# One small DRAM-to-DRAM copy put ahead of the first load of an instance-norm kernel

## The chip, the cores and the metric

The kernel runs on one core of a Trainium2 chip. The metric is the device time of one execution in microseconds (us). Three runs of the kernel before gave 627.54, 626.73 and 627.55 us, so the median is 627.54 us. The profile is one further execution, recorded by the hardware profiler.

A core has four computing engines that matter here: TensorE (PE), VectorE (DVE), ScalarE (ACT) and GpSimd (POOL). A fifth, SyncE (SP), only issues transfers. Transfers between device memory (DRAM) and the on-chip memory are carried by 16 DMA engines. SP, ACT and POOL can each put transfers into a queue of their own; all queues are served by the same 16 DMA engines.

## The reference: what is computed

```python
def reference(x, gamma):
    B, G, C_per_g, H, W = x.shape            # 4, 8, 16, 256, 256, float32
    mu = x.mean(axis=(3, 4), keepdims=True)
    var = ((x - mu) ** 2).mean(axis=(3, 4), keepdims=True)
    x_norm = (x - mu) / np.sqrt(var + 1e-5)
    out = x_norm * gamma[None, :, :, None, None]
    return out.astype(np.float32)
```

There are 4 x 8 x 16 = 512 channels of 256 x 256 = 65,536 numbers. Each channel is normalized by its own mean and variance and multiplied by one number of gamma. The input is 134.2 MB and so is the output; each has to cross between DRAM and the chip once.

## The kernel before, in words

The input is cut into 32 units (`U`). A unit is 16 channels. Each channel is spread over 8 partitions (`S`), 8,192 numbers in each, so a unit is a tile of 128 partitions by 8,192 float32 numbers: 4 MB, 32 KB in a partition. In DRAM a unit is one contiguous stretch of 4 MB.

Six tiles of that size, the slots `xt0` to `xt5` (line 45), hold the units that are in flight (`AHEAD = 6`). A unit is loaded into a slot, normalized there in place, and stored from there.

At the start, the gamma vector is loaded by POOL (line 52). Then the first six units are loaded (lines 53 and 54, through `load`, line 47): units 1 and 3 by the ACT queue, units 0, 2, 4 and 5 by the SP queue. A few constants are made: the averaging matrix `navg` on POOL, and `g_col`, gamma spread over the partitions, by DVE and PE.

The loop from line 100 takes the units in order. For each unit:

- DVE sums each partition (line 102), while ACT sums the squares of each partition (line 103).
- PE adds the sums over the 8 partitions of each channel and divides by the size (line 111).
- Four tiny operations turn that into the factor `scale` (lines 112, 116, 120, 122).
- DVE subtracts the mean and multiplies, in place (line 125).
- ACT issues the store of the unit to `out` (line 129).
- SP issues the load of the unit six places later into the same slot (line 131). It has to wait until the store from that slot has landed.

The order of instructions on each engine is the order in which they are written (`manual_schedule`, line 43). The waits between engines are put in by the framework, from what each instruction reads and writes, DRAM tensors too. The ACT and SP transfers share eight completion semaphores in turn. A transfer that reuses a semaphore waits until the transfer that used it before has landed.

Of the kernel before, what the change touches and what calls it, by code (L numbers as in the profile page):

```python
# [1 line left out]

# [4 lines left out]

F32 = mybir.dt.float32
U8 = mybir.dt.uint8
ALU = mybir.AluOpType  # L10
ACTF = mybir.ActivationFunctionType
AX = mybir.AxisListType


@with_exitstack
def kernel(
    ctx: ExitStack,
    tc: tile.TileContext,
    x: bass.AP,
    gamma: bass.AP,  # L20
    out: bass.AP,
):
    nc = tc.nc
    B, G, C, H, W = x.shape
    P = nc.NUM_PARTITIONS
    HW = H * W
    n_ch = B * G * C
    S = 8
    K = P // S
    F = HW // S  # L30
    U = n_ch // K
    NG = (G * C) // K
    AHEAD = 6
    assert HW % S == 0 and (G * C) % K == 0

    xv = x.rearrange("b g c h w -> (b g c h w)").rearrange("(u p f) -> u p f", p=P, f=F)
    ov = out.rearrange("b g c h w -> (b g c h w)").rearrange("(u p f) -> u p f", p=P, f=F)
    gv = gamma.rearrange("g c -> (g c)")

    data = ctx.enter_context(tc.tile_pool(name="data", bufs=1))  # L40
    singles = ctx.enter_context(tc.tile_pool(name="singles", bufs=1))
    psum = ctx.enter_context(tc.tile_pool(name="psum", bufs=4, space=bass.MemoryType.PSUM))
    ctx.enter_context(tc.manual_schedule())

    slots = [data.tile([P, F], F32, name=f"xt{i}") for i in range(AHEAD)]

    def load(u, queue):
        queue.dma_start(out=slots[u % AHEAD][:], in_=xv[u])  # L48


    g_row = singles.tile([1, G * C], F32, name="g_row")
    nc.gpsimd.dma_start(out=g_row[:], in_=gv[None, :])  # L52
    for u in range(AHEAD):
        load(u, nc.scalar if u in (1, 3) else nc.sync)


    eps_t = singles.tile([P, 1], F32, name="eps_t")
    nc.gpsimd.memset(eps_t[:], 1e-5)  # L58
    one = singles.tile([1, 1], F32, name="one")
    nc.gpsimd.memset(one[:], 1.0)  # L60
    navg = singles.tile([P, K, S], F32, name="navg")
    nc.gpsimd.memset(navg[:], -1.0 / HW)  # L62
    nc.gpsimd.affine_select(  # L63
        out=navg[:], in_=navg[:], pattern=[[-S, K], [0, S]], compare_op=ALU.is_ge,
        fill=0.0, base=0, channel_multiplier=1,
    )
    nc.gpsimd.affine_select(  # L67
        out=navg[:], in_=navg[:], pattern=[[S, K], [0, S]], compare_op=ALU.is_ge,
        fill=0.0, base=S - 1, channel_multiplier=-1,
    )  # L70
    navg_w = navg[:].rearrange("p k s -> p (k s)")
    root_eps = singles.tile([P, 1], F32, name="root_eps")
    nc.scalar.activation(out=root_eps[:], in_=eps_t[:], func=ACTF.Sqrt)  # L73
    g_rep = singles.tile([1, NG, K, S], F32, name="g_rep")
    g_ps = psum.tile([P, NG], F32, name="g_ps", bufs=1)
    g_col = singles.tile([P, NG], F32, name="g_col")

    nc.vector.tensor_copy(  # L78
        out=g_rep[:],
        in_=g_row[:].rearrange("o (n k) -> o n k", n=NG).unsqueeze(3).to_broadcast([1, NG, K, S]),  # L80
    )
    for n in range(NG):
        nc.tensor.matmul(  # L83
            out=g_ps[:, n : n + 1],
            lhsT=g_rep[:, n].rearrange("o k s -> o (k s)"),
            rhs=one[:],
            start=True, stop=True,
        )
    nc.vector.tensor_copy(out=g_col[:], in_=g_ps[:])  # L89

    junk = singles.tile([P, F], U8, name="junk")

    st = singles.tile([P, U, 2], F32, name="st")
    nvar = singles.tile([P, U], F32, name="nvar")
    std = singles.tile([P, U], F32, name="std")
    rstd = singles.tile([P, U], F32, name="rstd")
    scale = singles.tile([P, U], F32, name="scale")

    squares = []
    for u in range(U):  # L100
        t = slots[u % AHEAD]
        nc.vector.reduce_sum(out=st[:, u, 0:1], in_=t[:], axis=AX.X)  # L102
        square = nc.scalar.activation(  # L103
            out=junk[:], in_=t[:], func=ACTF.Square, accum_out=st[:, u, 1:2],
        )
        if u:

            tc.declare_no_dep(square.ins, squares[-1].ins, reason="junk, ordered by the root between")
        squares.append(square)
        ps = psum.tile([P, 2], F32, name="ps")  # L110
        nc.tensor.matmul(out=ps[:], lhsT=navg_w, rhs=st[:, u], start=True, stop=True)  # L111
        nc.vector.tensor_scalar(  # L112
            out=nvar[:, u : u + 1], in0=ps[:, 0:1], scalar1=ps[:, 0:1],
            scalar2=ps[:, 1:2], op0=ALU.mult, op1=ALU.add,
        )
        nc.scalar.activation(  # L116
            out=std[:, u : u + 1], in_=nvar[:, u : u + 1], func=ACTF.Sqrt,
            bias=eps_t[:], scale=-1.0,
        )
        nc.vector.reciprocal(out=rstd[:, u : u + 1], in_=std[:, u : u + 1])  # L120
        g = u % NG
        nc.vector.tensor_mul(  # L122
            out=scale[:, u : u + 1], in0=rstd[:, u : u + 1], in1=g_col[:, g : g + 1],
        )
        nc.vector.tensor_scalar(  # L125
            out=t[:], in0=t[:], scalar1=ps[:, 0:1], scalar2=scale[:, u : u + 1],
            op0=ALU.add, op1=ALU.mult,
        )
        nc.scalar.dma_start(out=ov[u], in_=t[:])
        if u + AHEAD < U:  # L130
            load(u + AHEAD, nc.sync)


# [1 line left out]
_INS = ['x', 'gamma']  # L135
_OUTS = [((4, 8, 16, 256, 256), 'float32')]


# [23 lines left out]
```

## Time and profile before

| What | Value |
|---|---|
| Median of three runs | 627.54 us (626.73 to 627.55) |
| Span of the profiled execution, first to last instruction | 625.2 us |
| Median time less that span | 2.3 us |
| Bytes moved by all DMA engines | 268.46 MB |
| Mean rate over the span | 429 GB/s |
| Busy: DVE, ACT, PE, POOL | 443.2, 238.8, 21.4, 1.9 us |
| First loads issued (SP and ACT) | 0.81 us |
| First unit on the chip, DVE begins | 22.76 us |
| First store issued | 37.82 us |
| Last store issued | 600.59 us |

The profile gives no time of the profiled execution other than its span, so the span is what the profile is compared by; the median of the unprofiled runs lies 2.3 us above it.

The profile is read in microseconds from the start of the span. A group row names the line, the engine, the operation, what is written from what, how often it ran, its total and mean time, and the idle time of that engine just before it with what ended it. A row of the stretches view gives, for each stretch of the span, its length, the busy time of each engine, the granted TensorE clock, the share of time in which the DMA engines were busy, and the rate. A DMA packet is put down to the stretch in which it starts. A packet of this kernel is 32 KB, one partition of a unit, so stretches of one or two us are uneven by that alone.

### The profile page before, as it was taken

To read this page: it belongs to the slowest core of one execution; us is meant where nothing else is said; L and a number is where in the kernel's file an instruction comes from. 1 tells how busy PE (TensorE), PEld (TensorE's weight loads), DVE (VectorE), ACT (ScalarE), POOL (GpSimd) and SP (SyncE) were. 2 spreads that over 40 slices of the span, in tenths; PEclk is the share of its full clock that TensorE was granted. 3 is DMA by queue.
4 is the path that set the end of the run, shared out by engine and by line. 5 is a ranking of instruction groups with operands and counts; after the bars stand their busy time and mean duration, and the time that the engine had idled before them with its cause. 6 is when DMAs were issued, how large, how long until landed. Compare 5 with 4: busy or idle time off the path is not lost.

```text
span 625.2 us, 627 instructions
## 1 busy us (share of the span) xinstructions
PE 21.4 (3%) x80; PEld 19.6 (3%) x80; DVE 443.2 (71%) x162; ACT 238.8 (38%) x98; POOL 1.9 (0%) x10
## 2 busy tenths in 40 slices
PE   2000000000000000000000000000000000000000
PEld 2000000000000000000000000000000000000000
DVE  0588999999776687666786767867668676687730
ACT  0444444444443244432344423444224442244400
POOL 1000000000000000000000000000000000000000
DMA  8999999999999999999999999999999999999998
GB/s 369 436 403 436 436 436 436 436 426 432 434 434 436 424 434 436 436 434 436 436 421 434 434 434 432 432 434 436 436 434 436 436 419 434 434 436 432 432 434 369
DMA packets 9251, 268.46 MB, mean 429 GB/s; under 512 B 1057, under 2 KB 1057, under 8 KB 1057
## 3 DMA queue, kind: packets, MB, share of 16 engines
q10 hardware_dynamic: 4896, 142.61, 52.9%
q1 hardware_dynamic: 4320, 125.83, 46.8%
q14 instruction: 3, 0.02, 0.0%
q0 software_dynamic: 32, 0.00, 0.0%
HBM read 134.22 MB, written 134.22 MB: 429 GB/s over the span
## 4 chain that ended last, share of the span: by engine, by line
another core or an unknown queue 61%; DMA 17%; DVE 15%; SPq 1%; PE 1%; issue 0%; ACT 0%
DMA xt<-in_x_dram 10%; DVE st L102 10%; DMA out_dram<-xt 8%; DVE xt L125 5%; SPq L48 1%; PE ps L111 1%; ACT std L116 0%; DVE nvar L112 0%; DVE rstd L120 0%; DVE scale L122 0%
## 5 line engine op out<-in xcount | busy, mean ns | idle before, releaser
L102 DVE TENSOR_REDUCE st<-xt 128x1 f32<-128x8192 f32 x32 | 277.9, 8684 | 105.3 <-DMA xt<-in_x_dram 105.3
L103 ACT ACTIVATE junk<-xt 128x8192 uint8<-128x8192 f32 x32 | 224.9, 7029 | 275.4 <-DMA xt<-in_x_dram 232.2
L125 DVE TENSOR_SCALAR xt<-xt,ps,scale 128x8192 f32<-128x8192 f32 x32 | 145.6, 4550 | 1.2
L116 ACT ACTIVATE std<-nvar,eps_t 128x1 f32<-128x1 f32 x32 | 9.4, 294 | 79.7 <-DVE nvar L112 79.7
L111 PE MATMUL ps<-st,navg 128*128 128x2 f32 x64 | 17.9, 349 | 562.0 <-DVE st L102 562.0
L111 PEld LDWEIGHTS ps<-st,navg 128*128 128x128 f32 x64 | 16.1, 312 | 563.8 <-issue 563.8
L112 DVE TENSOR_SCALAR nvar<-ps 128x1 f32<-128x1 f32 x32 | 9.2, 287 | 23.9 <-PE ps L111 23.9
L120 DVE RECIPROCAL rstd<-std 128x1 f32<-128x1 f32 x32 | 5.3, 164 | 11.6 <-ACT std L116 11.6
L78 DVE COPY g_rep<-g_row 1x1024 f32<-1x1024 f32 x1 | 0.7, 683 | 10.6 <-DMA g_row<-in_gamma_dram 10.6
L103 ACT ACTIVATION_READ_ACCUMULATOR junk<-xt 128x1 f32 x32 | 6.0, 186 | 0.0
L122 DVE TENSOR_TENSOR scale<-rstd,g_col 128x1 f32<-128x1 f32 x32 | 5.1, 159 | 1.1
L83 PE MATMUL g_ps<-one,g_rep 1*128 1x1 f32 x16 | 3.5, 347 | 11.5 <-DVE g_rep L78 11.5
L83 PEld LDWEIGHTS g_ps<-one,g_rep 1*128 1x128 f32 x16 | 3.5, 326 | 11.4 <-issue 11.4
L89 DVE COPY g_col<-g_ps 128x8 f32<-128x8 f32 x1 | 0.2, 167 | 3.7 <-PE g_ps L83 3.7
L73 ACT ACT_TABLE_LOAD x1 | 1.3, 1283 | 1.7 <-PEq L146 1.7
L52 POOL DMA_DIRECT2D g_row<-in_gamma_dram x1 | 0.6, 607 | 0.8 <-POOLq L146 0.8
L63 POOL TENSOR_SCALAR_AFFINE_SELECT navg<-navg 128x128 f32<-128x128 f32 x1 | 0.4, 398 | 0.1
L67 POOL TENSOR_SCALAR_AFFINE_SELECT navg<-navg 128x128 f32<-128x128 f32 x1 | 0.4, 398 | 0.1
L62 POOL MEMSET navg<- 128x128 f32 x1 | 0.2, 230 | 0.0
L73 ACT ACTIVATE root_eps<-eps_t 128x1 f32<-128x1 f32 x1 | 0.2, 203 | 0.0
L58 POOL MEMSET eps_t<- 128x1 f32 x1 | 0.1, 118 | 0.0
L146 POOL MEMSET const-bfloat16-1.0<- 128x1 bf16 x1 | 0.1, 102 | 0.0
(4 smaller groups left out, 0.4 us busy)
## 6 DMA issues: line engine op xcount, KB each, us to landing
out_dram<-xt ACTq DMA_DIRECT2D x32, 4096.0 KB, 62.5
xt<-in_x_dram SPq DMA_DIRECT2D x30, 4096.0 KB, 38.5
xt<-in_x_dram ACTq DMA_DIRECT2D x2, 4096.0 KB, 31.8
g_row<-in_gamma_dram POOLq DMA_DIRECT2D x1, 0.5 KB, 9.3
```

What stands on the lines that cost most here:

```text
L48: queue.dma_start(out=slots[u % AHEAD][:], in_=xv[u])
L73: nc.scalar.activation(out=root_eps[:], in_=eps_t[:], func=ACTF.Sqrt)
L78: nc.vector.tensor_copy(out=g_rep[:], in_=g_row[:].rearrange("o (n k) -> o n k", n=NG).unsqueeze(3).to_broadcast([1, NG, K, S]),)
L83: nc.tensor.matmul(out=g_ps[:, n : n + 1], lhsT=g_rep[:, n].rearrange("o k s -> o (k s)"), rhs=one[:], start=True, stop=True,)
L102: nc.vector.reduce_sum(out=st[:, u, 0:1], in_=t[:], axis=AX.X)
L103: square = nc.scalar.activation(out=junk[:], in_=t[:], func=ACTF.Square, accum_out=st[:, u, 1:2],)
L111: nc.tensor.matmul(out=ps[:], lhsT=navg_w, rhs=st[:, u], start=True, stop=True)
L112: nc.vector.tensor_scalar(out=nvar[:, u : u + 1], in0=ps[:, 0:1], scalar1=ps[:, 0:1], scalar2=ps[:, 1:2], op0=ALU.mult, op1=ALU.add,)
L116: nc.scalar.activation(out=std[:, u : u + 1], in_=nvar[:, u : u + 1], func=ACTF.Sqrt, bias=eps_t[:], scale=-1.0,)
L120: nc.vector.reciprocal(out=rstd[:, u : u + 1], in_=std[:, u : u + 1])
L122: nc.vector.tensor_mul(out=scale[:, u : u + 1], in0=rstd[:, u : u + 1], in1=g_col[:, g : g + 1],)
L125: nc.vector.tensor_scalar(out=t[:], in0=t[:], scalar1=ps[:, 0:1], scalar2=scale[:, u : u + 1], op0=ALU.add, op1=ALU.mult,)
```

## The change

One transfer is added on the SP queue, ahead of its first load. It reads 16 pieces of 2 KB (512 numbers of each eighth partition row) from the first unit of `x` and writes them to the same places of the first unit of `out`. Nothing is computed from them. The first store, issued by ACT, writes the whole first unit of `out`, and so overwrites the pieces; as it writes the same DRAM bytes it now also waits for the copy. Nothing else is changed in the source.

```diff
     g_row = singles.tile([1, G * C], F32, name="g_row")
     nc.gpsimd.dma_start(out=g_row[:], in_=gv[None, :])
+    nc.sync.dma_start(out=ov[0][0::S, 0:512], in_=xv[0][0::S, 0:512])
     for u in range(AHEAD):
         load(u, nc.scalar if u in (1, 3) else nc.sync)
```

In the built program, SP has one instruction more, its first. The order of all other instructions on all engines is the same. The transfers of ACT and SP use the eight semaphores one place further on. The first store has one wait more.

## The prediction

> **What bounds the kernel now.** I read the page's busy shares and its 40 slices first, then the queues, the groups, the waits of the SP queue, and stretches of the span around the start and the first store. From the page:
>
> ```profile
> PE 21.4 (3%) x80; PEld 19.6 (3%) x80; DVE 443.2 (71%) x162; ACT 238.8 (38%) x98; POOL 1.9 (0%) x10
> DMA  8999999999999999999999999999999999999998
> GB/s 369 436 403 436 436 436 436 436 426 432 434 434 436 424 434 436 436 434 436 436 421 434 434 434 432 432 434 436 436 434 436 436 419 434 434 436 432 432 434 369
> q10 hardware_dynamic: 4896, 142.61, 52.9%
> q1 hardware_dynamic: 4320, 125.83, 46.8%
> ...
> L102 DVE TENSOR_REDUCE st<-xt 128x1 f32<-128x8192 f32 x32 | 277.9, 8684 | 105.3 <-DMA xt<-in_x_dram 105.3
> ...
> out_dram<-xt ACTq DMA_DIRECT2D x32, 4096.0 KB, 62.5
> xt<-in_x_dram SPq DMA_DIRECT2D x30, 4096.0 KB, 38.5
> xt<-in_x_dram ACTq DMA_DIRECT2D x2, 4096.0 KB, 31.8
> g_row<-in_gamma_dram POOLq DMA_DIRECT2D x1, 0.5 KB, 9.3
> ```
>
> The DMA engines are busy in every slice; DVE, the busiest computing engine, has 71% and waits for loads. The bytes set the time. What stands out is how few slices fall short of 434 to 436 GB/s: the first, the last, and the third (403), with no computing reason for the third. The stretches view looks closer:
>
> ```profile
> 0.00:1.50 1.50, 0.00 (x0) 0.00 (x0) 0.00 (x0) 0.00 (x0) 0.42 (x5) 1.00 0.00 0
> ...
> 35.00:40.00 5.00, 0.00 (x0) 0.00 (x0) 5.00 (x2) 1.78 (x1) 0.00 (x0) 1.00 1.02 433
> 40.00:44.00 4.00, 0.00 (x0) 0.00 (x0) 4.00 (x1) 4.00 (x1) 0.00 (x0) 1.00 1.07 377
> ...
> 300.00:500.00 200.00, 6.14 (x22) 5.52 (x22) 143.66 (x55) 76.67 (x33) 0.00 (x0) 1.00 1.00 433
> ```
>
> No byte moves in the first 1.5 us. Between 40 and 44 us the rate falls to 377 with the engines "busy" all along: packets take longer there. The timeline has the first store at 37.82 us, just ahead:
>
> ```profile
> 37.82 0.35 ACTq L129 DMA_DIRECT2D out_dram<-xt  x1
> ```
>
> The views sum the packet records; I took the records themselves (start and duration of each 32 KB packet; 8,192 of them, 512 rounds of one packet on each of 16 engines), turned to the span's clock and sorted by start, 16 to a round:
>
> ```
> round   earliest  latest   mean start (us)
> 0       1.811     2.950    2.183     first load packets, took 1.21 to 2.10 us
> 1       3.655     4.213    3.868
> 2       4.872     5.420    5.090
> 31      39.968    40.517   40.186    first store packets, took 1.21 to 2.08 us
> 32      41.461    42.166   41.761    load packets behind them, 1.38 to 2.14 us
> 33      43.272    43.878   43.483
> 511     621.717   622.676  622.180   took 1.21 us
> ```
>
> A round lasts 1.2095 us in the median. Two places lose time: from round 0 to 1, 1.685 us were taken (0.48 over); from round 31 to 33, 3.297 us (0.88 over, on every engine between 0.88 and 0.94). All 512 rounds are over by only 1.94 us together. So the time is 1.8 us until the first packet, 512 x 1.2095 = 619.3 us of packets, these stalls, the spread of the engines, and 1.3 us from the last packet's end (623.89) to the end of the span.
>
> **The change part by part.**
>
> Bytes. 16 pieces of 2 KB are one packet on each engine. At 32 KB in 1.21 us a piece is 0.08 us; read and written it is 0.15 at most.
>
> Issue on SP. The first four loads took SP 0.37, 0.43, 0.42 and 0.53 us to issue, so the copy pushes all of them 0.37 to 0.53 us back. The ACT load of unit 1 is issued at 0.81 us as before and feeds the engines meanwhile; later loads stand in rings that are never empty: 0. Were that cover gone, the price would be those 0.4 us once.
>
> New wait. The first store (37.82 us) waits for a copy issued at 0.81. Behind it on ACT stand the squares of unit 1, and SP's reload of slot 0. Even the slowest small transfer in the trace, gamma's 0.5 KB behind the loads, landed after 9.3 us; so the wait is over 27 us before it is asked for: 0. The semaphores shift by one place, but each transfer still follows the same predecessor (a store the store four before, a load an early load, the first reload the copy instead of a fresh semaphore); at the end too, the last stores wait as before: 0.
>
> The first-store stall. It is the first time that an engine writes to `out`, and no later store repeats it (the rounds after 33 take 1.20 to 1.24 us; the second store, issued at 52.76, shows nothing). I take it for the price of a first write to `out`, which the copy pays in its place: -0.88 us. Bounds: 0 if it is the price of mixing stores into loads, -0.94 as the largest seen.
>
> The start. Here the copy stands ahead of the loads, and no row shows a DRAM-to-DRAM packet. Before, the slowest engine ran as if it had begun at 3.00 us (its third packet at 5.42 less two rounds); the first load packets start spread over 1.14 us, from 1.81 to 2.95, which I read as a 128-row load being handed out row by row. The copy has 16 rows, so I let it begin on all engines at 1.81. It holds an engine for a first read (the earliest load packet was 1.896 long, 0.68 over), the first write (0.88) and the bytes (0.15): 1.71 us, until 3.52. Loads then start 0.52 us later than on the slowest engine before: +0.52. Bounds: 0, if loads pass the copy's stalled write or its hold is under 1.19; and the two longest packets of the trace in a row, 2.10 + 2.14 = 4.24, until 6.05: +3.05. I take the value between, as a piece of 2 KB waits for the same first accesses but has a sixteenth of their data.
>
> The Trainium skill, page "DMA: Bandwidth & Descriptors", section "Anatomy of one DMA — SWDGE (gpsimd) path", speaks against the change: any transfer has a fixed cost of about 2.0 us, mostly the wait for the memory's receipt of the last write. If all of that held the engines, the copy would last until 3.81 and the sum would be about -0.07; the same page's section "Rules for kernel authors" lets such a cost overlap with other work. No run here shows a copy's own yet.
>
> Sum: +0.52 - 0.88 = -0.36 us on a span of 625.2, so 624.8. The median of the runs lies 2.3 above the span (launch and end, untouched): 627.54 - 0.36 = 627.2.
>
> **The rivals.**
>
> *The copy hides in the wait for descriptors and takes the loads' first stall too (faster).* For it: half of the engines stood idle until 2.5 to 2.95 us, and the late ones had no stall in their first packet (1.21 us). Then 0.88 and 0.48 both go: -1.36, 626.2. Against it: the late engines set the end, and those lost nothing at the start; the gain would need load descriptors that come no later than before.
>
> *The copy holds the engines and cures nothing (slower).* Place: 1.8 to 4.8 us. The stall at 40 us belongs to the first packet that is read on chip and written to DRAM, so it stays; and the copy's packet takes as long as the longest first load, 2.10, with 0.88 behind it: until 4.79, +1.79, 629.3. It passes 0.2% (1.25 us, about what a measurement of this kernel can tell from no change) once the hold is over 2.44 us. For it: in the trace an engine's slow store packet also slows the load packet behind it, so a stalled write does block the engine. Against it: the copy does write DRAM, on the same 16 engines.
>
> *The stall stays, the copy is cheap (no change).* +0.52 by the hold above, 628.1. If the stall belonged to each unit's stretch of `out`, every store would show it, and only the first does; so this needs the first mixing of stores and loads as its cause, but they alternate for hundreds of further rounds without loss.
>
> **How the numbers follow.** The forecast has 0.50, its own range 626.6 (-0.94) to 627.9 (a hold of 2.0 and the spread of the medians, 0.8, shared to both sides). The faster rival has 0.17, the slower 0.20, the cheap copy without cure 0.13. Over 0.2% is below 626.3 or above 628.8. Faster: 0.17 and 0.03 of the forecast's low edge, 0.20. Slower: 0.20, with 0.02 of each of the other two, 0.24. Within: 0.56. The range runs from 626.0, just below the faster rival, to 629.1, which leaves out about half of the slower rival and the tail toward 630.6 (+3.05), together under 2 in 10.
>
> **What would show it.** In the profile after: the third slice back at some 430 GB/s or more and the stretch from 40 to 44 us (or the four us after the first store) at 433 instead of 377, if the first write was moved; packets of rounds 31 and 32 at 1.21. At the start, the copy's issue on SP, loads behind it about 0.4 us later, first unit on the chip some 0.5 us after 22.76. No wait of the first store on the copy. A landing of the copy after more than 2.5 us, or loads whose second round starts after 4.7, speaks for the slower rival. What would make me wrong: a copy that stalls an engine far longer than any packet here, or a stall at 40 us that no early write to `out` can take away.

## The result, and the profile after

The changed kernel has a median of 627.8 us (22 executions) against 627.2 us for the kernel before (22). The ratio of the two is 1.0023, with a 95% interval from 1.0013 to 1.0032. It is slower: the whole interval lies above 1. I had forecast 0.36 us less than before.

The medians differ by 0.6 us, and the ratio stands for 1.4 us, because the executions of the changed kernel spread in a way those of before do not. Its 22 have a mean of 628.55, those of before 627.12. Sixteen of them lie at 627.19 to 628.23, with a mean of 627.61 (0.49 over before), and six at 628.71 to 633.23, with a mean of 631.06. So of the 1.43 us between the means, 0.49 are the everyday loss, paid by the sixteen, and 0.94 come from the six, the tail. The highest of before's 22 is 627.55.

The profiled execution took 627.39 us, so it is one of the sixteen. From its page:

```profile
span 625.7 us, 629 instructions
...
PE 21.4 (3%) x80; PEld 19.5 (3%) x80; DVE 443.1 (71%) x162; ACT 238.9 (38%) x98; POOL 1.9 (0%) x10
...
GB/s 371 436 415 421 436 436 436 436 436 429 434 432 430 429 429 436 434 434 436 434 436 436 432 434 432 432 432 432 432 436 432 436 434 436 434 434 432 436 432 354
...
L103 DVE TENSOR_REDUCE st<-xt 128x1 f32<-128x8192 f32 x32 | 277.9, 8684 | 104.2 <-DMA xt<-in_x_dram 104.2
...
out_dram<-xt ACTq DMA_DIRECT2D x32, 4096.0 KB, 69.8
xt<-in_x_dram SPq DMA_DIRECT2D x30, 4096.0 KB, 30.3
xt<-in_x_dram ACTq DMA_DIRECT2D x2, 4096.0 KB, 26.9
out_dram<-in_x_dram SPq DMA_DIRECT2D x1, 32.0 KB, 7.8
g_row<-in_gamma_dram POOLq DMA_DIRECT2D x1, 0.5 KB, 7.2
```

The compute rows are what they were. The dent in the rate has not gone: it was in the third slice (403 GB/s) and is now spread over the third and the fourth (415 and 421), because the first store comes later. The copy itself landed 7.8 us after its issue. The last slice is lower, 354 instead of 369. The stores now take 69.8 us from issue to landing, not 62.5, and the SP loads 30.3, not 38.5: the backlog has moved from one queue to the other. The stretches view of the changed kernel around the first store:

```profile
35.00:40.00 5.00, 0.56 (x2) 0.50 (x2) 3.82 (x5) 0.34 (x2) 0.00 (x0) 1.00 0.97 419
40.00:44.00 4.00, 0.00 (x0) 0.00 (x0) 4.00 (x2) 0.62 (x1) 0.00 (x0) 1.00 0.97 418
44.00:49.00 5.00, 0.00 (x0) 0.00 (x0) 5.00 (x1) 5.00 (x1) 0.00 (x0) 1.00 1.06 393
300.00:500.00 200.00, 6.14 (x22) 5.51 (x22) 143.78 (x55) 74.48 (x31) 0.00 (x0) 1.00 1.00 434
```

The slow stretch is now 44 to 49 us (393 GB/s), right behind the issue of the first store. The timeline shows why it is there:

```profile
0.81 0.59 SPq L53 DMA_DIRECT2D out_dram<-in_x_dram  x1
0.82 0.87 ACTq L48 DMA_DIRECT2D xt<-in_x_dram  x2
...
1.46 2.25 SPq L48 DMA_DIRECT2D xt<-in_x_dram  x4
...
27.92 8.69 DVE L103 TENSOR_REDUCE st<-xt 128x1 f32<-128x8192 f32 x1 [14.87 <-DMA xt<-in_x_dram]
...
42.98 0.35 ACTq L130 DMA_DIRECT2D out_dram<-xt  x1
```

SP is 0.59 us busy with the copy, so ACT issues its load of unit 1 first, 0.6 us ahead of SP's load of unit 0. Unit 0 is on the chip at 27.92 us instead of 22.76, and the first store is issued at 42.98 instead of 37.82: both 5.2 us later. In the timeline before, both queues begin at once (SP's row takes in a reload that comes much later, hence its length):

```profile
0.81 0.89 ACTq L48 DMA_DIRECT2D xt<-in_x_dram  x2
0.81 62.13 SPq L48 DMA_DIRECT2D xt<-in_x_dram  x5
...
22.76 8.69 DVE L102 TENSOR_REDUCE st<-xt 128x1 f32<-128x8192 f32 x1 [7.55 <-DMA xt<-in_x_dram]
```

The packet records of the trace tell the rest. Sorted by start into rounds of one 32 KB packet per engine (times in us, mean start of the round), with the number of the 16 packets that belong to SP's queue:

```
          before                         after
round   start    of SP's queue        start    of SP's queue
0       2.183    16                   2.151    0
1       3.868    0                    4.083    0
2       5.090    16                   5.303    0
4       7.515    16                   7.819    0
30      38.977   16                   39.281   16
31      40.186   0  last of loads     40.491   16
33      43.483   0  first store       42.915   16
35      45.902   0                    45.338   16  first store next
36      47.112   16                   47.056   7
37      48.321   0                    48.423   9
100     124.649  16                   124.795  7
511     622.180  0                    622.294  0
```

Before, all 16 engines do the same thing in the same round: all load for SP, then all carry out ACT's packets (loads at first, stores later), and so on through the span. ACT's two loads are 256 packets, 16 on each engine, and fill its rounds up to 31. After, each engine takes five packets of ACT's queue first; the copy, one packet of 2 KB and 0.084 us on each engine, does not move before 6.05 us. ACT's two loads are used up with round 26, and rounds 27 to 35 are SP's alone. When the first store arrives, some engines take its packets one round sooner than others, and from then on 7 engines load while 9 store, and the other way round in the next round. I call that out of step; how many engines are in each group is the split.

The rounds also correct a reading of my prediction. Its round 31, put down as "first store packets", holds the last load packets of ACT's queue; the first store's packets begin in round 33 and take 1.21 us. So the stall of 0.88 us falls on load packets, in the two rounds ahead of the first store's. It does so in the other kernels too: in gap_no_copy, below, the slow rounds 30 and 31 (0.31 and 0.86 us too long) have no packet of ACT's queue at all. I go on calling it the stall of the first store, as it comes right ahead of that store's packets in all 16 profiles (0.57 to 1.18 us); what makes it is not shown.

### The profile page after: what moved, and what is told of

It reads as the page before. It is cut to its first block, busy times and chain, and to the rows that moved or that the text cites. A ratio compares the mean times of both kernels' runs of the same rounds, so it can differ in the third digit from the quotient of the medians.

```text
span 625.7 us, 629 instructions
## 1 busy us (share of the span) xinstructions
PE 21.4 (3%) x80; PEld 19.5 (3%) x80; DVE 443.1 (71%) x162; ACT 238.9 (38%) x98; POOL 1.9 (0%) x10
## 4 chain that ended last, share of the span: by engine, by line
DMA 50%; DVE 25%; another core or an unknown queue 18%; PE 1%; issue 0%; ACT 0%; SPq 0%
DMA xt<-in_x_dram 43%; DVE st L103 19%; DMA out_dram<-xt 8%; DVE xt L126 5%; PE ps L112 1%; ACT std L117 0%; DVE nvar L113 0%; SPq L48 0%; DVE rstd L121 0%; DVE scale L123 0%; SPq L53 0%
## 6 DMA issues: line engine op xcount, KB each, us to landing
out_dram<-xt ACTq DMA_DIRECT2D x32, 4096.0 KB, 69.8
xt<-in_x_dram SPq DMA_DIRECT2D x30, 4096.0 KB, 30.3
```

## The experiments

The first theory was that the *head start* of ACT's load harms, by the late unit 0. Its rivals were that the *copy itself* costs, wherever it is issued, and the *first-write* reading of my prediction. In all diffs, `for u in range(AHEAD)` is the loop of the first loads.

**The copy on POOL's queue (pool_copy).**

```diff
-    nc.sync.dma_start(out=ov[0][0::S, 0:512], in_=xv[0][0::S, 0:512])
+    nc.gpsimd.dma_start(out=ov[0][0::S, 0:512], in_=xv[0][0::S, 0:512])
```

> The same 16-piece copy, issued by POOL behind gamma instead of by SP; the first transfers of SP and ACT are as in the kernel before. Head-start theory (the copy harms by making SP's load of unit 0 come behind ACT's load of unit 1): unit 0 on the chip at 22 to 23.5 us, the stall of the first store (about 0.8 us) still there, time within 0.3 us of the kernel before, no executions of 630 us or more. Rival (a DRAM-to-DRAM copy costs by itself): 0.5 us or more over the kernel before, and some executions at 630 to 633 us as with the change. My prediction's first-write theory: the stall of the first store is gone, 0.9 us under the kernel before.

Measured: 626.92 us against 626.9, ratio 0.9998 (0.999 to 1.0007), highest execution 627.44. Unit 0 is on the chip at 22.70 us, and the rounds are whole (16 or 0). The stall of the first store is still there, 0.77 us over rounds 31 and 32; in the stretches view:

```profile
40.00:44.00 4.00, 0.00 (x0) 0.00 (x0) 4.00 (x1) 4.00 (x1) 0.00 (x0) 1.00 1.10 393
```

The copy costs nothing that this run can see (at most 0.4 us, by the interval) by its bytes, by its write or by the first store's wait. The first-write reading falls: `out` was written early, at 12.1 us, and the stall is as before.

**The copy on ACT's queue (act_copy).**

```diff
-    nc.sync.dma_start(out=ov[0][0::S, 0:512], in_=xv[0][0::S, 0:512])
+    nc.scalar.dma_start(out=ov[0][0::S, 0:512], in_=xv[0][0::S, 0:512])
```

> The same copy as ACT's first transfer instead of SP's. Head-start theory: now SP's load of unit 0 gets into the engines first, so unit 0 is on the chip earlier than before, at 16 to 20 us instead of 22.8, and the first store is issued by 35 us; time within 0.5 us of the kernel before and no executions of 630 us or more. Rival (the copy or one more transfer ahead of the loads costs by itself, on whichever queue): 0.5 us or more over the kernel before, with executions at 630 to 633 us.

Measured: 627.26 us, ratio 1.0005 (0.9996 to 1.0014), 626.98 to 627.46. Now SP's load has the head start: unit 0 is on the chip at 18.01 us, the first store is issued at 33.07, and the rounds stay whole. As the head-start theory has it. The median is 0.36 us over that of before, and the interval allows up to 0.9.

**A small load instead of the copy (sp_small_load).** The pieces go to a part of the tile `junk`, which is made earlier for it; nothing is written to `out`.

```diff
-    nc.sync.dma_start(out=ov[0][0::S, 0:512], in_=xv[0][0::S, 0:512])
+    junk = singles.tile([P, F], U8, name="junk")
+    scratch = junk[0:16, 0:2048].bitcast(F32)
+    nc.sync.dma_start(out=scratch, in_=xv[0][0::S, 0:512])
```

> SP's first transfer is again 16 pieces of 2 KB from x, but into a tile on the chip, so nothing is written to out and no store waits for it. Head-start theory: the same as the change, unit 0 at some 27 to 28 us, median about 0.6 us over the kernel before, and some executions at 630 to 633 us. Rival (the DRAM-to-DRAM copy or the first store's wait costs): as the kernel before, within 0.3 us, unit 0 may be late but no executions of 630 us or more.

Measured: 643.25 us, 641.09 to 644.99 in four executions, ratio 1.026 (1.0241 to 1.028). Neither theory had that. The small load moves at once, at 1.81 to 2.68 us, where the copy moved at 6.05 in the same place of the same queue, and at 6.05 in act_copy too; so its place on the queue does not by itself explain the copy's wait, and what does is not shown. SP's load of unit 0 is issued 0.42 us behind ACT's, and ACT's first three packets, not five, come first on every engine. Unit 0 is on the chip at 25.49 us. Up to the first store (40.55 us) the rounds are whole and no slower than in the changed kernel; behind it, they mix, at 11 to 5 first and at changing splits from 104 us on. From the page of the execution at 641.09 us:

```profile
span 639.4 us, 629 instructions
...
GB/s 373 437 406 426 441 433 426 424 426 443 428 426 427 431 435 431 426 424 428 433 435 431 420 431 428 439 426 422 426 433 435 426 424 431 428 435 424 428 433 117
```

The rate is a little low through the whole span, and the last slice is nearly empty. In the packet records, load packets over 1.24 us (1.38 us in the median) come again and again, 284 of them between 80 and 560 us; the kernel before has two. Through them the engines drift apart: the first have done all their packets at 623.9 us, the last at 637.8. A transfer waits for its slowest engine, so the drift is the time.

That gave the second theory, *out of step*: what costs is that some engines load while others store, and the start matters only by what it does to the step.

**Unit 0 on the queue with the head start (unit0_act).** The change, with this:

```diff
-        load(u, nc.scalar if u in (1, 3) else nc.sync)
+        load(u, nc.scalar if u in (0, 2) else nc.sync)
```

> The change, with ACT loading units 0 and 2 and SP the copy and units 1, 3, 4 and 5. Head-start theory: ACT's first load has the head start again, but it is now unit 0, so unit 0 is on the chip at 16 to 20 us; time within 0.5 us of the kernel before, no executions of 630 us or more. Rival (the copy on SP costs by itself): as the change, 0.6 us over with executions at 630 to 633 us.

Measured: 627.38 us, ratio 1.0007 (0.9998 to 1.0016), 627.08 to 627.97 in 11 executions. The copy is where the change has it, SP's first transfer. In the timeline the first unit and the first store are early:

```profile
18.10 8.69 DVE L103 TENSOR_REDUCE st<-xt 128x1 f32<-128x8192 f32 x1 [5.16 <-DMA xt<-in_x_dram]
...
33.15 0.35 ACTq L130 DMA_DIRECT2D out_dram<-xt  x1
```

The rounds stay whole, and no execution is over 628 us. The tail is not seen with the copy kept, though 11 executions are few for a tail of 6 in 22. Whether the everyday loss has gone too, the run does not tell: the median is 0.48 us over the one beside it (626.9), and the interval holds no change as well.

**The same undoing for the small load (small_unit0).** sp_small_load with the same edit of the loop, units 0 and 2 on ACT.

> As sp_small_load (643 us), SP's first transfer is 16 pieces of 2 KB into a tile on the chip, but ACT now loads units 0 and 2, so that the first store comes at about 33 us while ACT's queue is still busy or just ends. Out-of-step theory: rounds stay whole (0 or 16 packets of SP's queue) behind the first store and the 16 us are gone: 627 to 628 us. Rival (the small on-chip load itself is what costs, by the SP queue or by its place on the chip): still over 635 us.

Measured: 627.35 us, 627.21 to 627.39 in 10 executions, ratio 1.0004 (0.9994 to 1.0013). First unit at 20.64 us, first store at 35.70, rounds whole. The 16 us are gone though the small load is still there.

**The change again (after_again, after_look1, after_look2, after_look3).** No edit.

> The changed kernel once more, for its spread and another profile. Out-of-step theory (the late first store finds ACT's queue empty and enters the 16 engines in different rounds, so that from then on some engines load while others store, and this costs from nothing to several us): the median 0.4 to 1 us over the kernel before, and one execution in four at 628.5 to 634 us; a profile in which rounds of packets after 45 us mix the two queues. Rival (the extra cost is a fixed price of the start): all executions within 1 us of each other.

> The change once more for one profile, in search of an execution of its slow tail. Out-of-step theory: a profile over 628.5 us has, after the first store, rounds that mix the queues in another split than 7 to 9, and load packets over 1.24 us again and again through the span (over 2 us in sum per engine); a fast one has none after 60 us. Rival (the tail comes from the start): a slow profile loses its time in the first 60 us.

> A second profile of the change, to find an execution of its slow tail. Expected as for the first look: if over 628.5 us, mixed rounds of another split than 7 to 9 and load packets over 1.24 us through the whole span (out-of-step theory), or a loss in the first 60 us alone (rival: the start).

> A third profile of the change, to find an execution of its slow tail. Expected as for the first look: if over 628.5 us, mixed rounds of another split than 7 to 9 and load packets over 1.24 us through the whole span (out-of-step theory), or a loss in the first 60 us alone (rival: the start).

Measured: 12 further executions have a median of 627.55 us, ratio 1.0012 (1.0 to 1.0025), 627.18 to 628.11 but for one at 632.37; the tail is there, but rarer than one in four. The profiles: 627.61 us with a split of 7 to 9, 627.25 with 10 to 6, 629.87 with 8 to 8, 627.68 with 3 to 13. So the split changes from execution to execution. In the one at 629.87 us there are 122 load packets over 1.24 us between 80 and 560 us, which make 0.8 us an engine in the mean (over 2 was expected); in the three others two each. Its engines end between 623.5 and 626.6 us, those of the one at 627.25 between 622.9 and 623.9. The stretches view of the end, first of the execution at 629.87 us:

```profile
60.00:615.00 555.00, 16.73 (x60) 15.02 (x60) 412.37 (x150) 220.66 (x90) 0.00 (x0) 1.00 1.00 432
...
621.00:624.00 3.00, 0.00 (x0) 0.00 (x0) 0.00 (x0) 0.00 (x0) 0.00 (x0) 1.00 0.84 360
624.00:626.00 2.00, 0.00 (x0) 0.00 (x0) 0.00 (x0) 0.00 (x0) 0.00 (x0) 1.00 0.15 66
```

and of the changed kernel's first profile, 627.39 us:

```profile
60.00:615.00 555.00, 16.72 (x60) 15.01 (x60) 412.51 (x150) 220.87 (x90) 0.00 (x0) 1.00 1.00 433
...
621.00:624.00 3.00, 0.00 (x0) 0.00 (x0) 0.00 (x0) 0.00 (x0) 0.00 (x0) 1.00 0.58 251
624.00:626.00 2.00, 0.00 (x0) 0.00 (x0) 0.00 (x0) 0.00 (x0) 0.00 (x0) 1.00 0.00 0
```

After 624 us the one still carries packets, the other none. The long execution has the marks of sp_small_load in small. That fits the out-of-step theory and not the rival, a loss in the first 60 us. But the long one has a split of 8 to 8 and the others 7 to 9, 10 to 6 and 3 to 13, and all four are out of step, three of them at no such price, so neither being out of step nor the numbers of the split tell which execution is costly. What the two long profiled executions share is the slow load packets and a split that does not last: at 629.87 us it leaves 8 to 8 at 263 us, while in the others the same pattern goes on to the last loads.

**An early store from the chip (pool_store).** In place of the copy, POOL writes zeros from a tile (`scratch`, made as in sp_small_load) to the same pieces of `out`.

```diff
-    nc.sync.dma_start(out=ov[0][0::S, 0:512], in_=xv[0][0::S, 0:512])
+    nc.gpsimd.memset(scratch, 0.0)
+    nc.gpsimd.dma_start(out=ov[0][0::S, 0:512], in_=scratch)
```

> No copy; POOL stores 16 pieces of 2 KB of zeros from a tile on the chip to out's first unit at the start; the first store overwrites them. If the stall at the first full store (about 0.8 us around 40 us) is the price of an engine's first write to out from the chip, it is gone here (under 0.2 us). If it is the price of the first mixing of full stores into full loads, it stays at 0.7 to 1 us. Time within 1 us of the kernel before either way.

Measured: one execution, 627.02 us. The stall stays: rounds 31 and 32 take 0.33 and 0.50 us too long, 0.83 in sum. So it is not the first write to `out` from the chip either. It comes with the first full store, or with something else that the small transfers do not share; which, was not settled.

**ACT's queue empty without a copy (gap_no_copy).** The kernel before, with ACT loading unit 1 alone.

```diff
-        load(u, nc.scalar if u in (1, 3) else nc.sync)
+        load(u, nc.scalar if u in (1,) else nc.sync)
```

> The kernel before without any copy, but ACT loads unit 1 alone and SP units 0, 2, 3, 4 and 5, so ACT's queue runs empty at about 21 us, long before the first store (about 38 us). Out-of-step theory: rounds after the first store mix the two queues (neither 0 nor 16 packets of SP's queue in a round), and the time is as with the change or worse: 0.5 us or more over the kernel before, with executions at 629 us or more. Rival (the copy, or the head start of unit 1, is what costs): the first unit arrives as before, within 1 us of 22.8, and the time is within 0.3 us of the kernel before with no executions over 629 us.

Measured: 627.56 us, ratio 1.0008 (1.0 to 1.0017), 627.28 to 627.83 in 11 executions. First unit at 22.51 us as before. The rounds mix, but only at 15 to 1, and there is no tail. The median is 0.57 over before, so about as much as the everyday part of the change's loss appears with no copy; the tail does not. The stall is longer here, 1.18 us instead of 0.88.

**A late first store without a copy (late_store).** The kernel before, with DVE held up by 5.3 us ahead of unit 0.

```diff
+    nc.vector.reduce_sum(out=st[:, 0, 0:1], in_=slots[0][:, 0:4900], axis=AX.X)
     squares = []
```

> The kernel before, with no copy and all transfers in their old order; DVE reduces 4,900 columns of unit 0 once more before it begins (about 5.2 us, its result is overwritten), so that the first store is issued at about 43 us as with the change, 3 us after ACT's queue has run out of loads. Out-of-step theory: the first store splits the engines, rounds after 45 us mix the queues, and the time is 0.3 to 1.5 us over the kernel before, with an execution over 628.5 us now and then. Rival (the copy or the head start of unit 1 costs): within 0.2 us of the kernel before, as DVE has the time to spare, and no tail.

Measured: 627.08 us, ratio 1.0003 (0.9994 to 1.0012), 626.73 to 627.29 in 11 executions. The first store comes at 42.99 us, as with the change; the engines split 15 to 1. Less than the 0.3 us that the out-of-step theory had put as its least, and no tail. A late first store finds the queue empty and splits the engines, as expected, but a split with one engine alone costs 0.2 us in the median here (up to 0.8 by the interval), against 0.57 in gap_no_copy. So a first store as late as the change's, with ACT's queue empty, did not by itself bring the change's loss in these 11 executions.

**ACT's queue kept full (copy_act_135).** The change, with ACT loading units 1, 3 and 5.

```diff
-        load(u, nc.scalar if u in (1, 3) else nc.sync)
+        load(u, nc.scalar if u in (1, 3, 5) else nc.sync)
```

> The change with its copy on SP, but ACT loads units 1, 3 and 5 and SP units 0, 2 and 4, so ACT's queue still holds loads (until about 54 us) when the first store comes at about 43 us. Out-of-step theory: the copy and the late first unit (27 to 29 us) are still there, but the rounds stay whole (0 or 16), there are no executions over 628.5 us, and the median is within 0.5 us of the kernel before. Rival (the copy or the late first unit costs by itself): as the change, with one execution in four at 628.5 to 634 us.

Measured: 627.31 us, ratio 1.0005 (0.9996 to 1.0014), 627.16 to 627.77 in 11 executions. Unit 0 is as late as with the change (27.92 us) and the first store enters whole rounds. The tail is not seen. But the rounds do not stay whole: now SP's queue runs empty (rounds 51 to 59 are ACT's alone), and from round 60, at 76 us, they mix at 7 to 9. In the profiled execution, 627.77 us, 22 load packets are over 1.24 us. So this run does not tell an early split from luck.

**The same for the small load (small_act_135).** sp_small_load with units 1, 3 and 5 on ACT.

> As sp_small_load (643 us), the small load into a tile on the chip as SP's first transfer and a late first unit (about 25 us or later), but ACT loads units 1, 3 and 5, so its queue still holds loads when the first store comes. Out-of-step theory: the rounds stay whole behind the first store and the time falls from 643 to under 630 us. Rival (the small load, or the late first unit, costs by itself): still over 635 us.

Measured: 627.35 us in the median of 10 executions, ratio 1.0015 (0.9999 to 1.0031); nine at 627.15 to 627.78, one at 632.75. First unit at 25.55 us, as late as in sp_small_load. The first store enters whole rounds and the 16 us are gone. Here too the rounds mix later (4 to 12, from 76 us), and one execution is in the tail. So neither the small load nor the late unit costs the 16 us, and a split that arises later can cost too.

All runs together:

```
rounds behind the first store      kernel          median   executions over 628.5 us
whole                              pool_copy       626.92   0 of 11
whole                              act_copy        627.26   0 of 11
whole                              unit0_act       627.38   0 of 11
whole                              small_unit0     627.35   0 of 10
mixed, 15 to 1                     gap_no_copy     627.56   0 of 11
mixed, 15 to 1                     late_store      627.08   0 of 11
whole to 76 us, then 7 to 9        copy_act_135    627.31   0 of 11
whole to 76 us, then 4 to 12       small_act_135   627.35   1 of 10
mixed, 7:9, 10:6, 8:8, 3:13        the change      627.80   6 of 22, then 1 of 12, 1 of 3
mixed, 11 to 5, then changing      sp_small_load   643.25   4 of 4
```

The splits are those of the profiled executions, and of those in the tail only two were profiled (629.87 and 641.09 us). In the kernels whose rounds are whole, or where one engine alone is out, no execution in 65 is in the tail. The kernels that have a tail are all among those with two larger groups. The kernel before, whole, had one execution at 629.01 among 27 that ran beside the first four experiments, so a long one is not impossible there either. So the table ties the tail to the larger splits but does not show that the split makes it. What the out-of-step theory leaves open is why most splits cost little and some up to 16 us: what makes the load packets slow. The records do not say which engine a packet ran on, so which engines are in a group, and what they share, was not tried.

## Why the prediction was wrong, step by step

Two steps failed. The sign of the forecast came from one of them, the -0.88 us for moving the stall of the first store, which is 0. The other is the issue on SP, priced at nothing: it changed the order of the queues.

**Bytes**: right. A piece took 0.084 us on its engine (0.08 was said).

**Issue on SP**: this step failed. The delay was near in size (0.59 us, 0.37 to 0.53 was said), and the cover was there, ACT's load of unit 1. I priced it at nothing because the engines had work. But the work was of the other queue: ACT's packets came first on all engines, five on each, unit 0 fell 5.2 us behind, ACT's queue ran out before the first store, and the engines went out of step. With copy and wait kept but the order untouched (pool_copy) the whole loss is absent, and with the copy kept on SP but unit 0 on ACT (unit0_act) the tail is, in 11 executions. The tail alone is 0.94 us of the 1.43. That the copy's place on SP's queue brings the loss, and not the copy, is what these runs show; how engines out of step then lose time stays open.

**New wait and semaphores**: right, nothing. The copy had landed at 8.6 us, 34 us ahead of the first store.

**The first-store stall, -0.88**: this step failed too; its true size is 0. Rounds 35 to 37 of the changed kernel, just ahead of the first store's packets and around them, are 0.51, 0.16 and 0.13 us too long, 0.80 in sum. Two other early writes to `out` left 0.77 and 0.83. The bound of 0 that I had named was the value. The records that I had could have warned me: the slow packets were loads, and the first store's own packets, from round 33 on, took 1.21 us.

**The start, +0.52**: wrong in mechanism and too large. The copy did not go first on the engines; it moved at 6.05 us, so it held nothing back at 1.8 us. In the five profiles of the changed kernel the fifth round begins 0.15 to 0.30 us later than before, 0.20 in the mean; 0.09 of it is the copy's own turn between rounds 2 and 3. The 2.0 us of fixed cost that the prediction cites stand there under the path of transfers that GpSimd issues; the copy, on SP, landed 7.8 us after its issue, but held an engine for 0.084 us only.

**The sum and the median**: I added 2.3 us from span to median, the profiled execution being one of the shorter ones. Here the profiled execution has 627.39 us on a span of 625.7, so only 1.7 lie outside it. The median of three that I predicted from, 627.54, is 0.3 above that of the 22 executions, 627.2.

So the terms I had come to +0.20 and 0 instead of +0.52 and -0.88. The everyday loss is 0.49 us. In the first profile of the change, whose span is 0.48 longer, the last packet ends 0.26 us later than before (624.15 instead of 623.89), and 0.22 us more pass between that and the end of the span (1.52 instead of 1.30). The later start has the size of the first part (0.30 us in this profile); the second was not looked into, and unit0_act and small_unit0, with whole rounds, have it too (1.53 and 1.52), so it does not come from being out of step.

**The rivals**: the slower one had the right sign by the wrong mechanism. It put the loss at 1.8 to 4.8 us and let it be the copy's hold; half of it, that the stall stays, was right. The sign that I had named for it, a landing of the copy after more than 2.5 us, came (7.8 us) without the hold. Its argument that a slow store packet slows the load behind it falls with the reading of round 31. The third rival, that the stall stays and the copy is cheap, had the right half too, and its 628.1 us is the nearest to the measured median of 627.8; that is luck, as its +0.52 was a hold that did not happen, and the tail was not in it. The faster rival counted half of the engines as idle until 2.5 us; in round 0 before, five of 16 were. That a change of queue order could put the engines out of step was among none of them, though the records that I had sorted into rounds could have shown all 16 engines in step.

## What to carry to other kernels

Where two queues feed the same DMA engines at full rate, a small transfer ahead of one queue's first load is not free because it is small: here it decided which queue was served first, and by that the order in which tiles arrived and when a queue ran empty. Sort the packet records into rounds and look whether the engines stay in step before pricing a delay as hidden. Compare distributions of executions, not one profile: the profile of this change looked nearly like the one before, and two thirds of its loss on average were in 6 of 22 executions.

## What the runs showed of the hardware

- The queue whose first load is issued 0.6 us ahead of the other's gets its first five 32 KB packets through on every engine ahead of the other's first (changed kernel, act_copy); 0.42 us ahead, its first three (sp_small_load); issued at the same time (0.81 us), the two alternate from the first packet (kernel before).
- Two queues with packets waiting alternate packet by packet, 1.2095 us each, and the engines kept a common step to the end of the loads in the kernels with whole rounds; they lost it where one queue had had no packets for some rounds (27 to 35 in the changed kernel) and then got packets again.
- Executions with the engines split into loading and storing groups took 627.39 us (7 to 9, the change) or 641.09 us (11 to 5 at first, sp_small_load); in the long one load packets take 1.25 to 2.4 us at times, and single engines end up to 14 us behind others.
- Right ahead of the first full store's packets, load packets lose time once, 0.57 to 1.18 us over two or three rounds in the 16 profiles, whatever small write to `out` came earlier; the store's own packets take 1.21 us.
